# Attention of a two-layer decoder trunk: transposed weights kept and 64 value columns streamed, the division by the sums put on the results, each pair of heads turned back by transposes

## The chip, the cores and the metric

The kernel runs on one NeuronCore of one Trainium2 chip. The metric is the device time of one execution in microseconds; the time before is the median of three runs. The engines are named as in the profile: PE is TensorE (its weight loads are PEld), DVE is VectorE, ACT is ScalarE, POOL is GpSimd, SP is SyncE.

## The reference

The program is a whole two-layer trunk on 512 tokens of width 1024. The change lies in the attention of layer 0 (8 heads, scores over 64 + 32 columns, 64 value columns a head, causal, in blocks of 128 queries):

```python
def mla_attention(qn, qr, kn, kr, v):
    S = qn.shape[1]
    scale = 1.0 / math.sqrt(QK_NOPE + QK_ROPE)
    outs = []
    for i in range(S // Q_BLOCK):
        q0, k_end = i * Q_BLOCK, (i + 1) * Q_BLOCK
        s = (jnp.einsum("bqhd,bkhd->bhqk", qn[:, q0:k_end], kn[:, :k_end])
             + jnp.einsum("bqhr,bkr->bhqk", qr[:, q0:k_end], kr[:, :k_end]))
        s = s.astype(jnp.float32) * scale
        mask = (q0 + jnp.arange(Q_BLOCK))[:, None] >= jnp.arange(k_end)[None, :]
        s = jnp.where(mask, s, jnp.finfo(jnp.float32).min)
        p = jax.nn.softmax(s, axis=-1).astype(v.dtype)
        outs.append(jnp.einsum("bhqk,bkhd->bqhd", p, v[:, :k_end]))
    o = jnp.concatenate(outs, axis=1)
    return o.reshape(o.shape[0], S, MLA_HEADS * V_HEAD)
```

Beside it runs a convolution module on 512 channels (gate, causal depthwise convolution of width 31, layer norm, swish). The two results, 512 channels each, are concatenated and mapped by one output projection. Then come a gated MLP, layer 1 (a pooling mixer and a second MLP) and a last norm.

## The kernel before

Activations are kept transposed: channels on the 128 partitions, the 512 tokens along the free dimension. Products with weights are made in three parts (`mm3`, L106 to L109): every fp32 operand is split into a high and a low half (`split`, L95 to L97: ACT casts the high half, DVE subtracts it to get the low one), and high × high, high × low and low × high are summed in one PSUM bank. The attention itself (L491 to L551) works in plain fp32.

For each head, `scores` (L491) makes four products, one for each block of 128 queries, 128 to 512 keys wide (L499). DVE adds the mask and takes the row maximum (L502), ACT takes the exponential and its row sum (L513), DVE takes the reciprocal of the four sums (L518), and ACT multiplies the four blocks of weights by it (L520). `transposes` (L524) turns the ten 128x128 blocks of weights on PE (L534), and ACT copies them out of PSUM into `pt` (L536), whose part j holds the weights of the keys in block j, turned, for all queries from block j on. `values` (L540) makes four products: the loaded operand is `vals[j]`, 128 keys by the 128 value columns of the head and its neighbour in the pair; the streamed one is part j of `pt`, 512, 384, 256 and 128 columns. The result has value columns on partitions and tokens along the free dimension. Of its 128 rows the 64 that belong to the head are split (L551) into its half of the pair's tile `att[hp]`.

The loop over heads (L572) interleaves three heads: scores of head h, transposes of h − 1, queries of h + 2 and values of h − 2. In between, `pump` hands out pieces of the depthwise convolution: a tap is either a product with a diagonal matrix on PE (L380) or a multiply-add on DVE (L387). After the loop stand the values of head 6, the first part of the output projection (`half`, L588; products with `att[0]` to `att[2]`), the transposes of head 7, more of the projection, and then the layer norm of the convolution's result: four rounds of transposes on PE (L612) into two banks used in turn, statistics on DVE (L614, L615), a copy on ACT (L617). The values of head 7 (L619) and the products with `att[3]` follow in the code, then rsqrt (L624, helper at L190), normalise (L626), four rounds of transposes back (L637), swish on ACT (L639) and the split, whose results enter the rest of the output projection.

That is the order in the code. The tile framework then orders the instructions of each engine itself by dependencies and its own costs, so the order on an engine differs from the code; each engine works through its own list in that order. PSUM results of the attention take banks in turn from a pool of six (`bank`, L82). The four closing copies of the convolution (`close`, L400 to L402) stand on ACT: the last, `side_876` before and after, is what the last transposes of each round at L612 read. Weights come by DMA in one stream (L121), and each arriving piece is split into halves by ACT and DVE (`prepare`, L142).

Of the kernel before, what the change touches and what calls it, by code (L numbers as in the profile page):

```python
# [8 lines left out]
F32 = mybir.dt.float32  # L9
F32R = mybir.dt.float32r  # L10
I32 = mybir.dt.int32
AF = mybir.ActivationFunctionType
# [3 lines left out]
P = 128  # L16
# [28 lines left out]
def kernel(  # L45
# [20 lines left out]
    act, dve, pool, pe = nc.scalar, nc.vector, nc.gpsimd, nc.tensor  # L66
# [11 lines left out]
    def uid(s):  # L78
        count[0] += 1
        return f"{s}{count[0]}"  # L80

    def bank():  # L82
        return p_ps.tile([P, S], F32, tag="ps", name=uid("ps"))

    def aux(tag="aux"):
        return p_ps.tile([P, S], F32, tag=tag, bufs=1, name=uid(tag))
# [4 lines left out]
    def small(n=4, dt=F32):  # L91
        return p_s.tile([P, 8], dt, tag=f"s{dt}", name=uid("s"))[:, :n]


    def split(dst, src):  # L95
        i = act.copy(dst[0], src)  # L96
        dve.tensor_tensor(dst[1], src, dst[0].bitcast(F32), op=ALU.subtract)  # L97
        return i
# [12 lines left out]
    def pair(t, lo=0, hi=S):  # L111
        return t[:, 0, lo:hi], t[:, 1, lo:hi]
# [4 lines left out]
    def rows_of(t, a, b):  # L117
        return t[a:b, 0, :], t[a:b, 1, :]
# [35 lines left out]
    def weights(ahead=1):  # L154
        given[0] += 1
        while len(ready) < min(given[0] + ahead, len(stream)):
            prepare()
        w = ready[given[0] - 1]
        ready[given[0] - 1] = None
        return w  # L160
# [4 lines left out]
    spare = p_s.tile([P, 1], F32, tag="spare", bufs=1, name="spare")  # L165
    dve.memset(spare, 1.0)
    act.activation(spare, spare, AF.Copy)
    ps = bank()
# [11 lines left out]
    ident, ones, fold_kr = sq[:, 0, :], sq[:, 1, :], sq[:, 2, :]  # L180
# [170 lines left out]
    def project():  # L351
        w = weights()
        ps = bank()
        for k in range(KD):
            mm3(ps, part(w, k), pair(xg[k]), k == 0, k == KD - 1)
        return ps
# [52 lines left out]
    def pump(nd, np_=0):  # L409
        for _ in range(min(np_, len(pe_work))):  # L410
            pe_work.pop(0)()
        for _ in range(min(nd, len(work))):
            work.pop(0)()
# [16 lines left out]
    def s4():  # L430
        return p_m.tile([P, 2, S], F32R, tag="s4", bufs=8, name=uid("s4"))
# [16 lines left out]
    ps = project()  # L448
# [14 lines left out]
    p_a = tc.alloc_tile_pool(name="attn", bufs=1, side="right", reuse_waits="tile")  # L463
# [13 lines left out]
    qs, probs, pts, sums, att = {}, {}, {}, {}, []  # L477
# [13 lines left out]
    def scores(h):  # L491
        q, key = qs.pop(h), keys[h // 2 % 2][:, h % 2, :]
        pb = p_a.tile([P, 1280], F32, tag="prob", bufs=3, name=uid("prob"))
        mx, nb, ls = small(), small(), small()
        blocks, at = [], 0
        for i in range(4):
            w = (i + 1) * P
            ps = bank()
            pe.matmul(ps[:, :w], q[:, i * P : (i + 1) * P], key[:, :w], start=True, stop=True)  # L499
            p = pb[:, at : at + w]  # L500
            at += w
            dve.tensor_tensor_reduce(  # L502
                out=p, in0=ps[:, :w], in1=causal[:, S - w :], scale=1.0,
                scalar=-3.0e38, op0=ALU.add, op1=ALU.max, accum_out=mx[:, i : i + 1],
            )
            blocks.append(p)
            if i % 2:
                two = slice(i - 1, i + 1)
                dve.scalar_tensor_tensor(
                    nb[:, two], mx[:, two], -1.0, q_scale[:, two], op0=ALU.mult, op1=ALU.mult  # L510
                )
                for n in (i - 1, i):
                    act.activation(  # L513
                        blocks[n], blocks[n], AF.Exp, bias=nb[:, n : n + 1],
                        scale=q_scale[:, n : n + 1], accum_out=ls[:, n : n + 1],
                    )
            pump(BLK, i % 2)
        dve.reciprocal(ls, ls)  # L518
        for i in range(4):
            act.activation(blocks[i], blocks[i], AF.Copy, scale=ls[:, i : i + 1])  # L520
        probs[h] = blocks
        sums[h] = ls[:, 3:4]

    def transposes(h):  # L524
        blocks = probs.pop(h)
        pt = p_a.tile([P, 1280], F32, tag="pt", bufs=2, name=uid("pt"))
        at, views = 0, []
        for js in ((0,), (1, 3), (2,)):
            ps = bank()
            n = 0  # L530
            for j in js:
                views.append((j, pt[:, at + n : at + n + S - j * P]))
                for i in range(j, 4):
                    pe.transpose(ps[:, n : n + P], blocks[i][:, j * P : (j + 1) * P], ident)  # L534
                    n += P
            act.copy(pt[:, at : at + n], ps[:, :n])  # L536
            at += n
        pts[h] = [v for _, v in sorted(views, key=lambda v: v[0])]

    def values(h):  # L540
        hp, e = h // 2, h % 2
        if e == 0:
            att.append(s4())
        ps = bank()
        for j, pt in enumerate(pts.pop(h)):
            pe.matmul(  # L546
                ps[:, j * P :], vals[j][:, hp * P : (hp + 1) * P], pt,
                start=j == 0, stop=j == 3,
            )
        a = e * 64  # L550
        split(rows_of(att[hp], a, a + 64), ps[a : a + 64, :])  # L551

    rows_kv = rows_tile()
    queries(0)
# [1 line left out]
    ps = bank()  # L556
# [7 lines left out]
    vals = []  # L564
    for j in range(4):
        ps = bank()
# [5 lines left out]
    for h in range(HEADS):  # L572
        scores(h)
        if h % 2 == 0 and h + 2 < HEADS:
            keys_of(h // 2 + 1)
        if h >= 1:
            transposes(h - 1)
        if h + 2 < HEADS:
            queries(h + 2)
        if h >= 2:  # L580
            values(h - 2)
        pump(END)
# [14 lines left out]

    last_sum = sums[HEADS - 1]
    values(HEADS - 2)
    w0 = weights()  # L600
    half(0, att, (0, 1, 2), True, w0)
    transposes(HEADS - 1)
    act.activation(spare, last_sum, AF.Silu)
    w1 = weights()
    half(1, att, (0, 1, 2), True, w1)

# [2 lines left out]
    for i in range(4):  # L609
        ps = aux(("aux", "conv")[i % 2])  # L610
# [6 lines left out]
        act.copy(yn, ps)  # L617
        yts.append(yn)
    values(HEADS - 1)  # L619
    half(0, att, (3,), True, w0)  # L620
    half(1, att, (3,), True, w1)
# [10 lines left out]
    for m in range(4):  # L632
        if m % 2 == 0:
            half(2, att, (m, m + 1), True, w2)
        ps = aux(("aux", "conv")[m % 2])
# [188 lines left out]
    for h in range(2):  # L824
        w = weights()
        for i in range(4):
            ps = aux("conv") if (h, i) == (0, 3) else bank()
# [10 lines left out]
            if (h, i) >= (0, 2):  # L838
                while zps:
                    i, ps = zps.pop(0)  # L840
# [7 lines left out]
    for m in range(KD):  # L848
        g, h = m // 2, m // 4
        ps = bank()  # L850
        for i in (0, 2, 1, 3):
            z = pair(zs[4 * h + i], (m % 4) * P, (m % 4 + 1) * P)
            q0 = min(i * P, 256)
            o = ps[:, q0 : q0 + 256]
# [136 lines left out]
```

## Time and profile before

| | before |
|---|---|
| median of 3 runs | 1016.07 us (1015.74 to 1018.9) |
| the profiled execution | 1015.51 us, span 1013.7 us |
| PE busy | 995.8 us of the span |
| DVE busy | 591.7 us |
| ACT busy | 399.7 us |
| granted TensorE clock | 0.996 |
| values, L546, 32 products | 64 passes of 128x512 to 128x128 |
| weight transposes, L534 | 80 |

The span is the time from the first to the last instruction on the core; the profiled execution's own time is 1.8 us longer. A group row of the profile gives line, engine, operation, tiles and shapes, the count, then busy time and mean of one, then the idle time before it and what ended most of that. The chain that ended last lists, for each piece of time, the instruction that the end waited for. Records of PE overlap, since an instruction's record lasts until its results are out, so what one costs in a stream is read from start to start.

### The profile page before, as it was taken

How to read it: one execution, taken by the hardware profiler on the slowest of the kernel's cores; microseconds unless marked ns; L12 is line 12 of the kernel's file. 1: busy time of each engine (PE TensorE's matmuls, PEld its weight loads, DVE VectorE, ACT ScalarE, POOL GpSimd, SP SyncE). 2: the span in 40 equal slices, each digit the busy share in tenths (PEclk: the TensorE clock that was granted, in tenths of full speed). 3: DMA queues.
4: the chain of work that ended last, by engine and by line, in shares of the span. 5: the costliest groups of instructions: out<-in, count | busy, mean ns of one | idle time of the engine just before them, and what ended most of it. 6: DMA issues, size and time to landing. Idle time of an engine off the chain costs nothing.

```text
span 1013.7 us, 11538 instructions
## 1 busy us (share of the span) xinstructions
PE 995.8 (98%) x4476; PEld 798.7 (79%) x4476; DVE 591.7 (58%) x914; ACT 399.7 (39%) x578; POOL 71.3 (7%) x107
## 2 busy tenths in 40 slices
PE   8999999999999999999999999999999999999996
PEld 6788676677888888888888889888888888888885
DVE  6999989856765555555332338485555555522323
ACT  6534677553433333333222246253333333232321
POOL 6000100022000000000000103100000000000111
PEclk9999999999999999999999999999999999999998
DMA  6432101113232232223232241322222223223212
GB/s 215 150 99 70 39 22 63 42 43 123 82 107 89 99 97 91 90 97 100 88 102 85 103 135 43 104 96 91 89 99 97 91 90 98 98 89 102 86 42 83
DMA packets 29478, 91.99 MB, mean 91 GB/s; under 512 B 4080, under 2 KB 6384, under 8 KB 29424
## 3 DMA queue, kind: packets, MB, share of 16 engines
q1 hardware_dynamic: 28880, 90.74, 27.3%
q8 instruction: 35, 0.57, 0.2%
q10 hardware_dynamic: 544, 0.52, 0.2%
q14 instruction: 19, 0.16, 0.0%
HBM read 89.02 MB, written 2.23 MB: 90 GB/s over the span
## 4 chain that ended last, share of the span: by engine, by line
PE 93%; DVE 4%; issue 1%; DMA 1%; SPq 0%; ACT 0%; DVEq 0%
PE ps L107 28%; PE ps L109 28%; PE ps L108 28%; PE ps L499 2%; PE ps L546 2%; DVE lo L97 1%; PE aux L380 1%; PE ps L534 1%; PE aux L248 1%; PE aux L226 1%; DVE xg L102 1%; DMA x<-in_xT_dram 0%; DMA col<-in_cols_dram 0%; PE ps L860 0%; PE ps L861 0%
## 5 line engine op out<-in xcount | busy, mean ns | idle before, releaser
L96 ACT CAST hi<-raw 128x1024 fp32r<-128x1024 f32 (+2 forms) x166 | 169.6, 1024 | 400.6 <-PE ps L108 373.0
L107 PE MATMUL ps<-xg,hi 128*128 128x512 f32 x816 | 324.6, 398 | 2.2 <-ACT hi L96 2.1
L109 PE MATMUL ps<-xg,lo 128*128 128x512 f32 x816 | 323.6, 397 | 1.4 <-DVE lo L97 1.4
L108 PE MATMUL ps<-xg,hi 128*128 128x512 f32 x816 | 323.8, 397 | 0.0
L97 DVE TENSOR_TENSOR lo<-raw,hi 128x1024 fp32r<-128x1024 f32 (+2 forms) x166 | 201.7, 1217 | 165.0 <-ACT hi L96 165.0
L107 PEld LDWEIGHTS ps<-xg,hi 128*128 128x128 f32 x816 | 153.9, 189 | 40.1 <-ACT hi L96 3.4
L109 PEld LDWEIGHTS ps<-xg,lo 128*128 128x128 f32 x816 | 153.7, 189 | 39.8 <-DVE lo L97 2.9
L108 PEld LDWEIGHTS ps<-xg,hi 128*128 128x128 f32 x816 | 153.9, 189 | 36.7
L107 PE MATMUL ps<-g,hi 128*128 128x512 f32 (+1 forms) x374 | 143.3, 383 | 0.0
L108 PE MATMUL ps<-g,hi 128*128 128x512 f32 (+1 forms) x374 | 143.1, 383 | 0.0
L109 PE MATMUL ps<-g,lo 128*128 128x512 f32 (+1 forms) x374 | 143.0, 382 | 0.0
L108 PEld LDWEIGHTS ps<-g,hi 128*128 128x128 f32 x374 | 70.4, 188 | 15.0
L109 PEld LDWEIGHTS ps<-g,lo 128*128 128x128 f32 x374 | 70.4, 188 | 15.0
L107 PEld LDWEIGHTS ps<-g,hi 128*128 128x128 f32 x374 | 70.4, 188 | 15.0
L687 DVE TENSOR_TENSOR t<-ps,rows 128x512 f32<-128x512 f32 x44 | 30.4, 691 | 83.8 <-PE ps L109 83.8
L699 DVE TENSOR_TENSOR t<-ps,rows 128x512 f32<-128x512 f32 x44 | 30.4, 690 | 75.0 <-PE ps L109 75.0
L213 POOL TENSOR_TENSOR sqr<-sqr,sqr 128x512 f32<-128x512 f32 x33 | 51.0, 1545 | 321.6 <-ACT sqr L211 291.5
L387 DVE SCALAR_TENSOR_TENSOR conv<-u,col,conv 128x512 f32<-128x512 f32 x90 | 67.5, 750 | 1.6 <-ACT conv L370 0.5
L694 DVE SCALAR_TENSOR_TENSOR t<-t,col,t 128x512 f32<-128x512 f32 x88 | 65.7, 748 | 1.4
L697 ACT ACTIVATE t<-t 128x512 f32<-128x512 f32 x44 | 27.8, 631 | 74.2 <-DVE t L694 74.2
L102 DVE SCALAR_TENSOR_TENSOR xg<-x,col,xg 128x512 fp32r<-128x512 f32 x32 | 32.7, 1038 | 12.1 <-ACT xg L101 12.1
L107 PE MATMUL ps<-s,hi 128*128 128x512 f32 x96 | 39.1, 421 | 0.0
(180 smaller groups left out, 812.9 us busy)
## 6 DMA issues: line engine op xcount, KB each, us to landing
raw<-in_w_up_dram SPq DMA_DIRECT2D x88, 512.0 KB, 3.3
raw<-in_w_down_dram SPq DMA_DIRECT2D x44, 512.0 KB, 3.2
raw<-in_w_in_dram SPq DMA_DIRECT2D x10, 512.0 KB, 3.3
raw<-in_w_out_dram SPq DMA_DIRECT2D x8, 512.0 KB, 3.3
x<-in_xT_dram SPq DMA_DIRECT2D x8, 256.0 KB, 4.2
raw<-in_w_in_dram SPq DMA_DIRECT2D x8, 256.0 KB, 3.6
raw<-in_w_uq_dram SPq DMA_DIRECT2D x4, 384.0 KB, 3.0
out_dram<-g SPq DMA_DIRECT2D x6, 256.0 KB, 2.6
```

The lines of the kernel that those rows point to most:

```text
L96: i = act.copy(dst[0], src)
L97: dve.tensor_tensor(dst[1], src, dst[0].bitcast(F32), op=ALU.subtract)
L102: dve.scalar_tensor_tensor(dst[1], src, scale, dst[0].bitcast(F32), op0=ALU.mult, op1=ALU.subtract)
L107: pe.matmul(ps, a[0], b[0], start=start, stop=False)
L108: pe.matmul(ps, a[0], b[1], start=False, stop=False)
L109: pe.matmul(ps, a[1], b[0], start=False, stop=stop)
L213: self.engine.tensor_tensor(self.parts[0], self.parts[0], t, op=ALU.add)
L387: i = dve.scalar_tensor_tensor(st["acc"], u[m][:, j : j + S], c(cw + j), st["acc"], op0=ALU.mult, op1=ALU.add,)
L687: dve.tensor_tensor(ut[:, 2 : 2 + S], pu, rows, op=ALU.mult)
L694: dve.scalar_tensor_tensor(a, ut[:, j : j + S], c(fw + j * NF + f), a, op0=ALU.mult, op1=ALU.add)
L697: act.activation(a, a, AF.Silu)
L699: dve.tensor_tensor(b, pv, rows, op=ALU.mult)
```

## The change

The weights are no longer multiplied by the reciprocal sums; they are turned unscaled. In `values` the loaded operand is now the 128x128 block of turned weights, and the streamed one the head's 64 value columns: ten products a head, one for each pair of a query block i and a key block j ≤ i, the products of one i summed in 64 columns of a bank. The result has tokens on partitions, so the reciprocal sum of a row is a per-partition scale, and ACT applies it while it copies the four results into the pair's tile `o`. After the second head of a pair PE turns `o` back by four transposes into one bank, and the pair is split once, at full height.

```diff
         dve.reciprocal(ls, ls)
-        for i in range(4):
-            act.activation(blocks[i], blocks[i], AF.Copy, scale=ls[:, i : i + 1])
         probs[h] = blocks
-        sums[h] = ls[:, 3:4]
+        sums[h] = ls
...
+    outs = {}
+
     def values(h):
+
+
         hp, e = h // 2, h % 2
         if e == 0:
+            outs[hp] = p_a.tile([P, 4, P], F32, tag="o", bufs=2, name=uid("o"))
+        o, pt, ls = outs[hp], pts.pop(h), sums[h]
+        ps = bank()
+        for i in range(4):
+            for j in range(i + 1):
+                pe.matmul(
+                    ps[:, i * 64 : i * 64 + 64], pt[j][:, (i - j) * P : (i - j + 1) * P],
+                    vals[j][:, h * 64 : h * 64 + 64], start=j == 0, stop=j == i,
+                )
+        for i in range(4):
+            act.activation(
+                o[:, i, e * 64 : e * 64 + 64], ps[:, i * 64 : i * 64 + 64], AF.Copy,
+                scale=ls[:, i : i + 1],
+            )
+        if e:
+            ps = bank()
+            for i in range(4):
+                pe.transpose(ps[:, i * P : (i + 1) * P], o[:, i, :], ident)
             att.append(s4())
-        ps = bank()
-        for j, pt in enumerate(pts.pop(h)):
-            pe.matmul(
-                ps[:, j * P :], vals[j][:, hp * P : (hp + 1) * P], pt,
-                start=j == 0, stop=j == 3,
-            )
-        a = e * 64
-        split(rows_of(att[hp], a, a + 64), ps[a : a + 64, :])
+            split(pair(att[hp]), ps)
...
-    act.activation(spare, last_sum, AF.Silu)
+    act.activation(spare, last_sum[:, 0:1], AF.Silu)
```

In the changed program the values are L550, the scaling L555, the turning back L562, and later lines stand 13 further down (the transposes of the convolution's rows are L625 instead of L612); `transposes` stands two lines higher (L532 and L534 instead of L534 and L536).

Since the framework orders the instructions anew, three places are shown as they stand in the two programs. The first is PE at the values of heads 5 and 6. Before, from the end of the transposes of head 6:

```order
L534 MATMUL ps_1597<-sq,prob_1477 128x128 x2
L546 MATMUL ps_1601<-pt_1518,v_967 128x512
L546 MATMUL ps_1601<-pt_1518,v_976 128x384
L546 MATMUL ps_1601<-pt_1518,v_985 128x256
L546 MATMUL ps_1601<-pt_1518,v_994 128x128
L546 MATMUL ps_1622<-pt_1584,v_967 128x512
L546 MATMUL ps_1622<-pt_1584,v_976 128x384
```

Now, from the ninth and tenth products of head 5 (`ps_1625`) on; `ps_1640` is the bank into which pair 2 is turned back, and `ps_1662` holds the values of head 6:

```order
L550 MATMUL ps_1625<-v_985,pt_1538 128x64
L550 MATMUL ps_1625<-v_994,pt_1538 128x64
L562 MATMUL ps_1640<-sq,o_1555 128x128
L550 MATMUL ps_1662<-v_967,pt_1608 128x64
L562 MATMUL ps_1640<-sq,o_1555 128x128
L550 MATMUL ps_1662<-v_967,pt_1608 128x64
L562 MATMUL ps_1640<-sq,o_1555 128x128 x2
L550 MATMUL ps_1662<-v_976,pt_1608 128x64
```

The four transposes of the pair stand between the first products of the next head. At pairs 0 and 1 the ten products of the second head are followed by one conv tap (L380) and then by the four transposes.

The second place is PE behind the values of head 7. Before, `ps_1785` and `ps_1635` to `ps_1680` are banks of the output projection, `s_1621` is `att[3]`:

```order
L546 MATMUL ps_1740<-pt_1655,v_976 128x384
L546 MATMUL ps_1740<-pt_1655,v_985 128x256
L546 MATMUL ps_1740<-pt_1655,v_994 128x128
L107 MATMUL ps_1785<-s_1220,hi_1675 128x512
L108 MATMUL ps_1785<-s_1220,hi_1675 128x512
L109 MATMUL ps_1785<-s_1220,lo_1676 128x512
L107 MATMUL ps_1785<-s_1392,hi_1675 128x512
L107 MATMUL ps_1635<-s_1621,hi_1376 128x512
L107 MATMUL ps_1636<-s_1621,hi_1376 128x512
L107 MATMUL ps_1679<-s_1621,hi_1631 128x512
L107 MATMUL ps_1680<-s_1621,hi_1631 128x512
L612 MATMUL aux_1700<-sq,side_454 128x128
```

Now, from the turning back on, which stands directly behind the ten products of head 7 (`att[3]` is `s_1808`):

```order
L562 MATMUL ps_1803<-sq,o_1661 128x128 x4
L107 MATMUL ps_1849<-s_1312,hi_1723 128x512
L108 MATMUL ps_1849<-s_1312,hi_1723 128x512
L109 MATMUL ps_1849<-s_1312,lo_1724 128x512
L107 MATMUL ps_1849<-s_1498,hi_1723 128x512
L107 MATMUL ps_1683<-s_1808,hi_1380 128x512
L107 MATMUL ps_1684<-s_1808,hi_1380 128x512
L107 MATMUL ps_1727<-s_1808,hi_1679 128x512
L107 MATMUL ps_1728<-s_1808,hi_1679 128x512
L108 MATMUL ps_1849<-s_1498,hi_1723 128x512
L109 MATMUL ps_1849<-s_1498,lo_1724 128x512
L625 MATMUL aux_1748<-sq,side_454 128x128
```

Two more matmuls of the projection stand ahead of the transposes of the convolution's rows, beside the four transposes of the pair.

The third place is ACT at the same point, with the engines that each row waits for. Before, from the copies of the turned weights of head 7 to the closing copy of the convolution:

```order
L536 COPY pt_1655<-ps_1656 128x512 [waits PE_49]
L536 COPY pt_1655<-ps_1662 128x512 [waits PE_49]
L536 COPY pt_1655<-ps_1668 128x256 [waits PE_49]
L96 CAST s_1621<-ps_1740 64x512 [waits PE_49]
L402 ACTIVATE side_876<-aux_1011,col 128x512 [waits DVE_49]
```

Now:

```order
L534 COPY pt_1703<-ps_1704 128x512 [waits PE_49]
L534 COPY pt_1703<-ps_1710 128x512 [waits PE_49]
L534 COPY pt_1703<-ps_1716 128x256 [waits PE_49]
L555 ACTIVATE o_1661<-ps_1788,s_1574 128x64 [waits PE_49]
L555 ACTIVATE o_1661<-ps_1788,s_1574 128x64 [waits Activation_49] x3
L96 CAST s_1808<-ps_1803 128x512 [waits PE_49]
L402 ACTIVATE side_876<-aux_1011,col 128x512 [waits DVE_49]
```

The four scalings have come in ahead of the cast, and only the first of them names PE.

## The prediction

> **What bounds the kernel now.** I read the page first: the engines' totals and the summary of the chain that ended last.
>
> ```profile
> PE 995.8 (98%) x4476; PEld 798.7 (79%) x4476; DVE 591.7 (58%) x914; ACT 399.7 (39%) x578; POOL 71.3 (7%) x107
> PE 93%; DVE 4%; issue 1%; DMA 1%; SPq 0%; ACT 0%; DVEq 0%
> ```
>
> TensorE bounds the whole; 93% of the chain is PE, 4% DVE. The change lies between the first and the last weighted sum of values, so I cut the span by stages (engine busy us; the table by stretches):
>
> ```profile
> 129.50:189.20 59.70, 59.70 (x258) 41.16 (x257) 55.52 (x120) 41.40 (x96) 3.62 (x6) 1.00 0.08 27
> 189.20:204.20 15.00, 12.90 (x66) 9.31 (x66) 11.13 (x29) 8.49 (x13) 0.10 (x1) 1.00 0.26 79
> 204.20:1013.70 809.50, 799.16 (x3595) 651.18 (x3594) 413.86 (x550) 282.08 (x355) 47.29 (x73) 1.00 0.28 92
> ```
>
> In the first stretch, the attention, PE is busy all 59.70 us at clock 1.00, with DVE close behind (55.52) and ACT at 41.40. In the second, the hand-over to the output projection, PE has 2.10 us of holes. A busy PE can hide waits, because records overlap, so I looked at the pitch from start to start, which the chain in order of time gives:
>
> ```profile
> 146.23 1.09 PE ps L534 x10
> 149.41 2.16 PE ps L546 x8
> 152.23 0.86 PE aux L380 x2
> ```
>
> Ten transposes take 1.09 us (0.109 each), one head's values 2.16, one conv tap 0.86. The same three figures come back for every head, with 0.23 for each weight matmul. So PE never waits in the attention: its time there is a sum of pitches, and each pitch added is added to the run. The third view is the chain behind the last values:
>
> ```profile
> 187.02 2.16 PE ps L546 x8
> 189.18 0.23 PE ps L107
> ...
> 189.87 1.17 PE ps L107 x5
> 191.04 0.44 PE aux L612 x4
> ...
> 194.20 1.02 DVE lo L97
> ...
> 199.72 0.56 DVE t L626
> ...
> 202.06 0.79 ACT t L639
> 202.85 0.04 issue
> 202.89 0.66 PE aux L637 x4
> ```
>
> Up to the first transposes of the conv rows (L612, 191.04) it is PE's own order. From there it runs over DVE (statistics, rsqrt, normalise) and ACT back to PE, and PE's other matmuls are only filler. So what moves L612 moves the end.
>
> **What leaves ACT and DVE.** The groups of ACT by form (count, busy us, mean ns of one):
>
> ```profile
> L520 ACT ACTIVATE prob<-prob,s 128x512 f32<-128x512 f32 x8 | 5.7, 711 | 0.0
> L520 ACT ACTIVATE prob<-prob,s 128x384 f32<-128x384 f32 x8 | 4.8, 603 | 0.0
> L520 ACT ACTIVATE prob<-prob,s 128x256 f32<-128x256 f32 x8 | 4.0, 497 | 0.0
> L520 ACT ACTIVATE prob<-prob,s 128x128 f32<-128x128 f32 x8 | 3.2, 402 | 0.7 <-DVE s L518 0.6
> L536 ACT COPY pt<-ps 128x512 f32<-128x512 f32 x16 | 8.6, 580 | 2.3 <-PE ps L534 2.3
> L536 ACT COPY pt<-ps 128x256 f32<-128x256 f32 x8 | 3.0, 371 | 0.0
> L570 ACT ACTIVATE v<-ps,s 128x512 f32<-128x512 f32 x4 | 2.7, 687 | 2.9 <-PE ps L109 2.9
> L96 ACT CAST hi<-raw 128x1024 fp32r<-128x1024 f32 x6 | 6.3, 1048 | 3.3 <-PE ps L108 3.3
> ```
>
> And from the timeline, four scalings in a row and the last head's split:
>
> ```profile
> 178.65 1.93 ACT L520 ACTIVATE prob<-prob,s 128x128 f32<-128x128 f32 x4
> 189.21 0.58 ACT L96 CAST s<-ps 64x512 fp32r<-64x512 f32 x1 [5.88 <-PE ps L546]
> 189.83 0.69 DVE L97 TENSOR_TENSOR s<-ps,s 64x512 fp32r<-64x512 f32 x1 [0.93 <-ACT s L96]
> ```
>
> The scaling of the weights goes: 5.7 + 4.8 + 4.0 + 3.2 = 17.7 us of ACT. Eight half-height splits become four of full height and 512 columns like these, so 4 × 0.58 of ACT and 4 × 0.69 of DVE go too. I value all of it at zero: PE waited for none of it (its pitches are whole). The sums that are now kept whole, and the copy that reads them at L603, cost nothing more. A gain below zero is excluded in the attention for that reason; in the hand-over the chain enters DVE only behind L612.
>
> **What PE gets for its values.** Before: 8 × 2.16 = 17.3 us. After, each head has ten products of 64 columns; in fp32 a product is two passes (the chain shows eight passes for four products), each loading 128 columns of transposed weights. So 160 passes. No row of the kernel before has 64 columns. The nearest below are the sums of squares, 128 columns loaded and only 2 streamed:
>
> ```profile
> 69.35 0.95 PE L226 MATMUL aux<-sq,sqr 128*128 128x2 f32 x8
> 70.15 0.48 PE L107 MATMUL ps<-xg,hi 128*128 128x512 f32 x1
> 70.47 0.40 PE L108 MATMUL ps<-xg,hi 128*128 128x512 f32 x1
> ```
>
> From the first start (69.35) to L108 (70.47) less one L107 pitch (0.23) are 0.89 us for 8 passes, 0.111 each. A pass that streams next to nothing costs as much as one transpose with 128 columns: the load sets the pitch. The chain itself books less, as the load of the next matmul then shows in the 0.32 us from L107 to L108:
>
> ```profile
> 69.51 0.79 PE aux L226 x8
> ```
>
> That is 0.099 each, the small end of the near rows. The far end: if only streamed columns counted, 512 + 384 + 256 + 128 = 1280 columns in two passes took 2.16 us, 0.84 ns a column and pass, so 64 columns 0.054 us. I take 0.111, as both a 2-column and a 128-column neighbour show about that. One head: 20 × 0.111 = 2.22, **+0.06 a head, +0.5 us** in all. The far end would be 20 × 0.054 = 1.08 a head, −8.6 us.
>
> [...]
>
> **The turning back.** 4 pairs × 4 transposes × 0.109 = **+1.7 us** on PE, by the pitch; one record is longer, since records overlap:
>
> ```profile
> L534 PE MATMUL ps<-sq,prob 128*128 128x128 f32 x80 | 10.0, 273 | 0.0
> ```
>
> They take one more of the six result banks a pair; PE waited for no bank before, so I put that at zero, and its price if the cover is gone is in the third rival. [...]
>
> **The new wait.** The transposes need the four scaled results. On ACT the first of the four waits for PE and the others do not, so I take it that it waits for the whole bank of values, not for its own 64 columns. Its price: L570 reads PSUM with a scale, 687 ns at 512 columns; the slope of the copies is (580 − 371)/256 = 0.82 ns a column, so 64 columns cost 0.32 us (estimate). Four in a row overlap as L520's do, (2.21 − 1.93)/3 = 0.09 each: 1.0 us. ACT starts 0.28 us after PE's stream has left the values (L107 started at 188.93, the cast at 189.21):
>
> ```profile
> 188.93 0.48 PE L107 MATMUL ps<-s,hi 128*128 128x512 f32 x1
> 189.82 0.69 ACT L402 ACTIVATE side<-aux,col 128x512 f32<-128x512 f32 x1
> ```
>
> and PE follows ACT by 0.04 (202.85 above). With E the end of the values on PE, the four results are there at E + 0.65, 0.88, 1.11, 1.33. Last pair: nothing stands between, the last transpose ends at E + 1.44 and holds 0.44 of work: 1.0 us lost. Pair 2: each transpose is followed by one product of the next head (0.22), so only the first wait is lost, 0.65. Pairs 0 and 1: a tap of 0.86 stands between; 0.15 each. Sum **+1.95 us**. Behind the waiting transposes everything on PE is queued. Bounds: 0.35 if each result waited for its own columns only, and 1.05 more a pair if a weight cast (1048 ns above) stood ahead on ACT.
>
> The cast of the last pair (E + 1.5 to 2.1) and the closing copy L402 (to 2.8) come behind on ACT; L612 stands on PE at E + 1.44 + 10 × 0.23 = 3.8. Both are covered by the matmuls between; with less than 1 us of them L402 would decide.
>
> **The order.** In the hand-over ten weight matmuls now stand between the values and L612 where eight stood: **+0.47 us** before the chain goes to DVE. The fillers behind are shorter by as much, but nothing waits for them.
>
> **Sum.** 0.5 + 1.7 + 1.95 + 0.47 = 4.6 us, carried unchanged through the third stretch, where PE is busy 799 of 809 us. The profiled execution took 1015.51 us (span 1013.7 and 1.8 around it), which becomes 1020.1. It lies 0.56 under the median of the runs, 1016.07; on that the forecast is **1020.7 us**, 0.45% slower. About 0.3%, 3 us, is what a measurement of this kernel can tell from no change.
>
> **Rivals.**
> - *Streamed columns set the pass, faster.* If loads hide behind other passes, values cost 1.08 a head: −8.6 + 1.7 + 1.95 + 0.47 = −4.5, 1011.6 us. It decides once a pass costs under 0.082 us (160 × 0.029 = 4.6). For it: 512- and 384-column passes hide their loads. Against: L226 at 0.111. Chance 0.06.
> - *The small ends, no change.* A pass at the 0.099 that the chain books (−1.4), transposes 1.7, half of the waits because ACT starts each result on its own columns, 1.0, order 0.47: +1.8, 1017.9 us. For it: the waits are estimates, and ACT has 18.3 us free in the 59.7. Chance 0.18.
> - *ACT's order makes it late, slower still.* If at each pair a cast or the exponentials stand ahead of the four scalings, each wait grows by about 1.05: +8.8, 1024.9. Against: ACT loses 17.7 us there and the casts stand beside the values' 2.2 us. DVE, in order too, stops at the pair's split until the cast is there, and the next scores' reduction waits behind it; its slack is 4.2 us. Chance 0.08.
> - That the change is not made is excluded: the order shows eighty products of 64 columns.
>
> The forecast keeps 0.68, with its own range from 1019.2 (waits 1.0, a pass a little cheaper) to 1022.4 (pairs 0 to 2 each 0.6 later). The range 1017.8 to 1023.0 takes in the second rival and leaves out the first and the third. Slower by over 0.3% means over 1019.1: 0.62 of the forecast's 0.68 and all of the third, 0.70. Within 0.3%: 0.06 and 0.18, 0.24. Faster: 0.06.
>
> **What would show it.** In the profile after: values of a head as 20 passes in 2.1 to 2.3 us from start to start; 16 transposes at 0.109; PE idle or stretched before them by about 1.0 at the last pair, 0.65 at the one before; L612 4 to 5 us later than 191.04 and the stretch behind it as long as before. Wrong if the values take under 1.7 us a head, if PE waits in the attention for DVE or for a free bank, or if the distance from L612 to the first output matmul of L639's results changes.

## The result and the profile after

The changed kernel takes 1021.86 us, median of 6 runs (1021.03 to 1022.52), beside 1015.81 us (1014.54 to 1018.9) for the kernel before on the same chip: ratio 1.0059, 95% interval 1.0048 to 1.0070. It is slower, as forecast, 1.2 us above the predicted 1020.7 and inside the range. The profiled execution took 1021.94 us with a span of 1020.1 us, 6.4 us more than before. One thing of single executions is needed below: the mean granted clock was 0.990 to 0.992 in five of the six executions after and 0.994 in one, while of the 79 executions of the kernel before that stood beside the experiments 63 had 0.993 to 0.997 (median 1016.1 us) and 16 had 0.991 (median 1018.2 us).

The engines' totals and the clock in 40 slices, from the page of the kernel after:

```profile
PE 1000.7 (98%) x4588; PEld 808.2 (79%) x4588; DVE 589.0 (58%) x910; ACT 390.3 (38%) x574; POOL 71.3 (7%) x107
PEclk9999999989999999999999999999999999999998
```

PE has 4.9 us more work, ACT 9.4 us less (by rows 17.7 us of scaling and 2.3 us of half-height casts gone, 7.4 us of scaled copies come in; rows overlap, so they don't add up to the total). The ninth slice, about 204 to 230 us, has an 8 where before there was none: the first thing that the forecast hadn't. The table by stretches, cut as before (attention, hand-over, rest):

```profile
129.30:192.50 63.20, 62.39 (x370) 49.54 (x368) 52.91 (x116) 36.35 (x101) 3.62 (x6) 1.00 0.08 26
192.50:208.60 16.10, 13.64 (x67) 10.21 (x67) 11.35 (x29) 8.65 (x14) 0.10 (x1) 0.91 0.26 78
208.60:1020.10 811.50, 801.12 (x3596) 651.96 (x3595) 413.60 (x550) 281.84 (x355) 47.36 (x73) 0.99 0.27 91
```

PE, full in the attention before, now has 0.81 us without work there, and the hand-over runs at a mean clock of 0.91. The chain in order of time shows the pieces:

```profile
129.43 2.18 PE ps L550 x20
...
141.82 0.44 PE ps L562 x4
...
174.00 2.19 PE ps L550 x20
176.22 0.32 ACT o L555
...
176.59 0.33 PE ps L562
...
189.19 2.19 PE ps L550 x20
191.41 0.32 ACT o L555
...
191.78 0.94 PE ps L562 x4
...
195.06 0.44 PE aux L625 x4
...
206.21 0.79 ACT t L652
...
207.04 1.12 PE aux L650 x4
```

Twenty passes of 64 columns take 2.18 us, where eight of up to 512 columns took 2.16. ACT's scaling is now in the chain at the last two pairs and not at the first two (141.82: four transposes in 0.44, no wait). The last line has four transposes in 1.12 us; before, the same four took 0.66.

To see where the time came in, I read four starts on PE in each trace: the first product of the values; the first transpose of the conv rows into the bank `aux` (L612 before, L625 after); the first transpose back (L637, L650); and the next sum of squares (L226), at about 256 us.

| distance, us | before | after | difference |
|---|---|---|---|
| first values to conv rows | 61.46 | 65.62 | +4.16 |
| conv rows to transposes back | 9.53 | 9.54 | +0.01 |
| transposes back to sum of squares | 55.37 | 57.71 | +2.34 |
| from there to the end | 757.9 | 757.9 | 0 |

So 4.16 us came in the attention and at its end, the chain over DVE is as long as it was, and 2.34 us came behind it, where the change has moved nothing. There the clock is seen in a table by stretches of the kernel after:

```profile
194.90:202.50 7.60, 7.60 (x40) 5.95 (x38) 6.21 (x16) 4.08 (x7) 0.00 (x0) 1.00 0.24 74
202.50:205.90 3.40, 1.59 (x8) 0.80 (x8) 3.16 (x12) 1.01 (x1) 0.00 (x0) 0.98 0.44 142
205.90:212.40 6.50, 5.84 (x19) 4.68 (x19) 3.48 (x5) 4.84 (x8) 0.10 (x1) 0.50 0.25 83
212.40:222.00 9.60, 9.60 (x43) 7.71 (x42) 0.00 (x0) 0.00 (x0) 0.00 (x0) 0.99 0.00 0
```

For 3.40 us PE has run out of projection matmuls and does a few transposes, busy 1.59 us; then TensorE is granted half its clock for 6.5 us. The nearest stretch of the profiled execution before is not answered so:

```profile
199.10:204.10 5.00, 2.90 (x18) 1.68 (x17) 3.59 (x9) 2.91 (x5) 0.10 (x1) 1.00 0.31 104
204.10:212.00 7.90, 7.90 (x36) 6.41 (x35) 2.54 (x4) 2.81 (x5) 0.00 (x0) 1.00 0.15 56
```

In this trace the granted clock is 1.00 or 0.50 and nothing else, and PE was not idle ahead of the lower one, busy 1.59 of 3.40 us. Whether the same hole could lose the clock in one execution and keep it in another is taken up behind the last experiments.

### The profile page after: what moved, and what is told of

Read it like the earlier page. It is cut to its first block, busy times and chain, and to the rows that moved or that the text cites. A ratio compares the mean times of both kernels' runs of the same rounds, so it can differ in the third digit from the quotient of the medians.

```text
span 1020.1 us, 11755 instructions
## 1 busy us (share of the span) xinstructions
PE 1000.7 (98%) x4588; PEld 808.2 (79%) x4588; DVE 589.0 (58%) x910; ACT 390.3 (38%) x574; POOL 71.3 (7%) x107
## 4 chain that ended last, share of the span: by engine, by line
PE 93%; DVE 4%; issue 1%; DMA 1%; SPq 0%; ACT 0%; DVEq 0%
PE ps L107 28%; PE ps L109 28%; PE ps L108 28%; PE ps L499 2%; PE ps L550 2%; DVE lo L97 1%; PE aux L380 1%; PE ps L532 1%; PE aux L248 1%; PE aux L226 1%; DVE xg L102 1%; DMA x<-in_xT_dram 0%; DMA col<-in_cols_dram 0%; PE ps L874 0%; PE ps L873 0%
## 5 line engine op out<-in xcount | busy, mean ns | idle before, releaser
L97 DVE TENSOR_TENSOR lo<-raw,hi 128x1024 fp32r<-128x1024 f32 (+2 forms) x166 | 201.7, 1216 | 165.0 <-ACT hi L96 165.0
```

## The experiments

My theory after the result: the load of the weights sets a pass with 64 columns streamed (0.109 us), as with 2 (0.111) and 128 (0.109) in the kernel before (values +0.6), 16 transposes cost 1.75, the last two pairs wait for ACT, two more matmuls stand ahead of the conv rows; and the rest is the clock, which falls because PE's hole in the hand-over got emptier. Rivals: the ACT relief or the width decides; the extra 2.3 us are not the clock but the new traffic of `o`; the hand-over's order, which the framework chose, is worth more than all the arithmetic of the change. Distances as in the table above, in us; each ratio is to runs of the kernel before on the same chip, whose median was 1015.81 to 1016.60 us, so ratios and distances compare across the table better than the medians do:

| kernel | median us (runs) | ratio to before, 95% | values to rows | rows to back | back to squares |
|---|---|---|---|---|---|
| e_noscale | 1015.89 (11) | 0.9998 (0.9989–1.0008) | 61.46 | 9.53 | 55.38 |
| e_nowait | 1022.62 (4) | 1.0059 (1.0044–1.0075) | 66.10 | 9.84 | 56.93 |
| e_late | 1019.94 (5) | 1.0036 (1.0023–1.0049) | 63.45 | 11.52 | 56.14 |
| e_fill | 1020.26 (5) | 1.0037 (1.0024–1.0049) | 65.64 | 9.45 | 55.46 |
| e_hole | 1017.35 (11) | 1.0010 (1.0001–1.0019) | 61.47 | 11.24 | 56.50 |
| e_wide | 1016.69 (10) | 1.0001 (0.9992–1.0010) | 59.68 | 11.37 | 56.12 |
| e_order | 1018.80 (10) | 1.0023 (1.0009–1.0038) | 61.38 | 11.46 | 56.13 |
| a_lo | 1018.69 (11) | 1.0022 (1.0013–1.0031) | 65.62 | 8.41 | 55.61 |
| a_both | 1018.09 (10) | 1.0019 (1.0005–1.0034) | 61.37 | 11.48 | 56.13 |
| b_lo | 1014.72 (11) | 0.9981 (0.9972–0.9990) | 61.46 | 8.41 | 55.61 |
| b_order | 1016.10 (10) | 0.9996 (0.9984–1.0008) | 60.25 | 11.34 | 56.13 |
| b_both | 1015.94 (10) | 0.9996 (0.9985–1.0007) | 60.25 | 10.32 | 56.12 |

**e_noscale: ACT's relief alone.** The kernel before without the scaling:

```diff
-        for i in range(4):
-            act.activation(blocks[i], blocks[i], AF.Copy, scale=ls[:, i : i + 1])
```

> The kernel before without the 32 scalings of the weights by the reciprocal sums on ACT (17.7 us of ACT); it leaves out the division. Theory: PE waited for none of them, so the time is that before within 0.3 us. Rival (the relief of ACT is worth something that the change then gives back): 1 us or more faster.

Every distance is that of before to 0.01 us, and the ratio 0.9998. Taking the 17.7 us of scalings off ACT (its total falls from 399.7 to 385.4 us) is worth nothing, as valued.

**e_nowait: the transposes without their wait.** In the kernel after, the turning transposes read a tile that has long been there:

```diff
-                pe.transpose(ps[:, i * P : (i + 1) * P], o[:, i, :], ident)
+                pe.transpose(ps[:, i * P : (i + 1) * P], vals[i][:, :P], ident)
```

> The changed kernel whose 16 turning transposes read the value tiles, long ready, in place of the scaled results; it leaves out the use of the attention's result behind the scaling. The framework puts 15 projection matmuls, not 10, ahead of the conv rows in the hand-over, so the stretches are to be read apart. Theory: from the first product of values to the last transpose of pair 3 the trace loses the 1.2 us of waits and keeps the 1.75 us of transposes at 0.109 each. Rival (the transposes themselves are dear, 0.2 us or more each, and nothing waits): that stretch stays as long as in the changed kernel.

The ratio is that of after, 1.0059, and the clock falls in the hand-over here too (0.50 in 206 to 212 us, 0.95 in the 6 us ahead). The expected loss is there, from the first values to the end of the last transpose 61.93 us instead of 63.45, but it doesn't reach the end. PE at the last pair, from the timeline of this kernel:

```profile
189.04 2.34 PE L550 MATMUL ps<-v,pt 128*128 128x64 f32 x20
191.22 0.61 PE L562 MATMUL ps<-sq,v 128*128 128x128 f32 x4
192.40 0.50 PE L107 MATMUL ps<-s,hi 128*128 128x512 f32 x1 [0.57 <-ACT o L555]
```

and in the kernel after:

```profile
189.03 2.34 PE L550 MATMUL ps<-v,pt 128*128 128x64 f32 x20
191.78 0.94 PE L562 MATMUL ps<-sq,o 128*128 128x128 f32 x4 [0.41 <-ACT o L555]
192.47 0.48 PE L107 MATMUL ps<-s,hi 128*128 128x512 f32 x1
```

The transposes follow the values at once, but the next matmul of the projection then stands behind ACT for almost as long: 192.40 instead of 192.47. At pair 2 the wait does go: from the first product of head 5 to the projection are 4.78 us (174.36 to 179.14) instead of 5.30 (173.84 to 179.14), that is 0.52 less. The order on PE changed with it, too: fifteen matmuls stand ahead of the conv rows instead of ten, 1.17 us, which eats the gain. So the wait at the last pair is not the transposes' alone; ACT's four copies cost it in either form, though which bank or tile the projection's matmul waits for was not followed.

**e_late: the transposes away from their wait.** The turning of pairs 0 and 1 comes after the next head's scores, that of pair 2 after the values of head 6, that of pair 3 behind the conv rows, and with it the products with `att[3]`:

```diff
+        if h >= 4 and h % 2 == 0:
+            turn(h // 2 - 2)
...
+    turn(2)
...
-    half(0, att, (3,), True, w0)
-    half(1, att, (3,), True, w1)
...
+    with tc.issue_after(behind_conv.ins):
+        turn(3)
+    half(0, att, (3,), True, w0)
+    half(1, att, (3,), True, w1)
```

> The changed kernel with each pair turned back later: pairs 0 and 1 after the next head's scores, pair 2 behind the values of head 6, pair 3 behind the last transposes of the conv rows, with the products that need it behind that. The framework then puts the transposes of the conv rows directly behind the values of head 7. Theory: the waits of the turning back (1.2 us), its last four transposes (0.44) and the ten projection matmuls ahead of the conv rows (2.3 us) leave the path, and the chain to the end starts some 3 to 4 us earlier; with a shorter hole no drop of the clock: 1016 to 1018 us. Rival: the matmuls that were fillers are now late and bound PE behind the chain, or the closing copy of the last conv row is not ready (DVE's taps): 1019 to 1021.

The conv rows come 2.17 us sooner (63.45 for 65.62) and the chain behind them is 1.98 longer. PE now waits for the closing copy of the convolution, which ACT makes behind the four scalings:

```profile
193.64 1.07 PE L629 MATMUL aux<-sq,side 128*128 128x128 f32 x4 [1.59 <-ACT side L402]
```

This is the cover that the prediction named ("with less than 1 us of them L402 would decide"), now gone: the 1016 to 1018 us that I expected were missed, and the rival of the closing copy came true. The clock falls right behind it, from the table by stretches:

```profile
193.90:200.70 6.80, 5.61 (x22) 4.81 (x21) 4.50 (x14) 2.83 (x5) 0.00 (x0) 0.51 0.00 0
```

**e_fill: work in the hole.** The kernel after, with thirty small bf16 matmuls on a tile of zeros issued ahead of the first transposes back:

```diff
+        if m == 0:
+            for _ in range(30):
+                pe.matmul(ps[:, :P], idle, idle, start=True, stop=True)
```

> The changed kernel with 30 small bf16 products of zeros put among PE's fillers of the hand-over (their result is overwritten by the transposes of the normalised rows), about 1.7 us of PE work that nothing waits for. Theory: 2.3 of the 6 us that the change costs are the TensorE clock, which the trace after grants at 0.50 from 205.9 to 212.4 us behind a longer hole of PE; with the hole filled the clock stays at 1.00 there, the mean clock goes back to 0.996, and the time falls by 1.8 to 2.3 us, to about 1019.7. Rival: the stretch is long because the four transposes and the first products wait for ACT and DVE; then the filler changes nothing (1021.9) or adds up to 1.7 us.

The framework put them ahead of the last projection matmuls, which so came later and filled the hole. The table by stretches of this kernel, over the same times:

```profile
202.00:205.90 3.90, 3.49 (x31) 2.74 (x28) 3.45 (x17) 0.00 (x0) 0.00 (x0) 1.00 0.79 251
205.90:212.40 6.50, 5.71 (x31) 4.17 (x30) 4.24 (x8) 5.88 (x9) 0.10 (x1) 1.00 0.26 83
```

Clock 1.00, and the distance behind the chain is 55.46, 2.25 less than after; its mean granted clock is 0.994 to 0.996 in all five runs. The median fell by 1.6 us, and the ratio from 1.0059 to 1.0037, which is 2.2 us. In its profiled execution the clock was low near the start, in 10 to 30 us (0.91), which the profiled execution after hadn't. So the 2.34 us are the clock to within 0.1 us, and the traffic of `o` is not needed to explain them.

**e_hole: the hole made in the kernel before.** One more DVE operation in the chain:

```diff
+    dve.tensor_scalar(yts[0], yts[0], 1.0, None, op0=ALU.mult)
```

> The kernel before with one more pass of DVE over the first of the four normalised rows (times 1.0), about 0.5 us in the chain from the statistics to the transposes, so that PE's hole there is as long as in the changed kernel. Theory of the clock: the hole, not the new way of making the values, drops the clock; the granted clock falls to 0.50 for some us behind it and the time grows by 0.5 + 2.3, to about 1018.6, mean clock about 0.992. Rival (the drop belongs to the new values and transposes): +0.5 us, 1016.3, and a mean clock of 0.996.

The operation's record is 0.42 us, yet the chain got 1.71 longer. In DVE's order it stands behind all four normalise steps (201.88, the first of them at 200.05), and the first transpose back, which could follow the first step before, now waits for it. So PE's hole is 3.01 us, longer than the 1.77 in the kernel after. The clock fell in the profiled execution, and for as long:

```profile
202.00:208.40 6.40, 5.93 (x22) 4.95 (x23) 3.02 (x5) 4.75 (x8) 0.10 (x1) 0.50 0.27 84
```

The median, 1017.35, is only 0.1% above before and 1.3 below the expected 1018.6, and only two of the eleven executions have the expected mean clock of 0.992. The trace shows the drop without the change, but before has such executions too, so how often the hole calls it up is not shown, and with the chain made longer at once the test doesn't price it.

**a_lo and b_lo: a shorter chain, in both.** In the chain between conv rows and transposes back, DVE also made the low halves of weights for the projection (the line `DVE lo L97` of the chain before). They now come behind the last normalise:

```diff
-        copied = split((hi, lo), raws[i])
+        copied = act.copy(hi, raws[i])
+        with ExitStack() as late:
+            if lo_after:
+                late.enter_context(tc.issue_after(lo_after[0]))
+            dve.tensor_tensor(lo, raws[i], hi.bitcast(F32), op=ALU.subtract)
```

> The kernel before with the low halves of the three weight tiles that are prepared in the hand-over taken by DVE behind the normalising instead of among the statistics; PE's order stays. Theory: the chain from the transposes of the conv rows (L612) to those back is bound by DVE's order, of which two splits of 1.2 us are part; without them it is up to 2.2 us shorter, then bound by PE's own fillers, so about 1.4 us go, the hole of PE closes and the clock cannot drop: about 1015, and no execution with the mean clock of 0.991. Rival (the splits are needed as soon for the products behind, or statistics wait for PE): no change.

> The same in the changed kernel. Theory: the chain is up to 2.2 us shorter and the hole closes, so that the clock stays at 1.00 behind it: 1.4 to 2.2 plus 2.3 us less than the changed kernel, 1017.5 to 1018.2. Rival (the drop of the clock does not hang on the hole): the gain stays under 2.2 us, 1019.7 or more.

The chain got 1.12 us shorter in both, 8.41 us, and behind it the clock is 1.00 in both traces; none of b_lo's eleven executions has a mean clock under 0.994. b_lo takes 1014.72 us, less than both kernels of this case and near the expected 1015. a_lo takes 1018.69, 0.5 above the expected range and 3.2 less than after; by the distances 1.13 are the chain and 2.10 the clock (55.61 for 57.71). With the clock thus alike, the change costs 1018.69 − 1014.72 = 3.97 us, and by the distances 4.16, all of it ahead of the conv rows: this is what the prediction's 4.6 us stood for.

**e_wide: 128 columns streamed.** The kernel after with the neighbour's columns streamed too and thrown away:

```diff
-                    ps[:, i * 64 : i * 64 + 64], pt[j][:, (i - j) * P : (i - j + 1) * P],
-                    vals[j][:, h * 64 : h * 64 + 64], start=j == 0, stop=j == i,
+                    ps[:, i * P : (i + 1) * P], pt[j][:, (i - j) * P : (i - j + 1) * P],
+                    vals[j][:, hp * P : (hp + 1) * P], start=j == 0, stop=j == i,
```

> The changed kernel with the 128 value columns of the pair streamed in each product in place of the head's 64, of which ACT still takes 64; the results are the same. Theory: the load of 128 columns sets a pass, so a head's 20 passes stay at 2.2 us from start to start. Rival (streamed columns set the pass, with some fixed cost): 64 more columns at 0.84 ns a column and pass, 1.1 us more a head, 8.6 us in all.

On the width the chain of this kernel is plain:

```profile
175.01 2.25 PE ps L550 x20
...
190.03 0.44 PE aux L625 x4
...
190.57 1.34 PE ps L550 x12
...
194.95 0.73 PE ps L562 x3
```

Twice the columns take 2.25 us instead of 2.18, where 1.1 us more were due if streamed columns set the pass: the load, 128 columns in both, sets it (0.112 and 0.109 us a pass). But the run as a whole is 5.2 us faster than after, level with before. The lines show what else is new: the conv rows (L625) now stand ahead of the values of head 7, and the projection's matmuls, which in the kernel after stood ahead, fill the chain behind them. The framework had chosen another order for the hand-over. That called for the next four.

**e_order, b_order, a_both, b_both: that order given to the others.** In the kernel after, before, a_lo and b_lo the values of head 7 are held behind the first round of conv rows:

```diff
+        if i == 0:
+            conv_row = behind_conv
...
-    values(HEADS - 1)
+    with tc.issue_after(conv_row.ins):
+        values(HEADS - 1)
```

> The kernel after (64 value columns) with its last head's values held behind the conv rows, which is the order on TensorE that the kernel with 128 columns had got; nothing else is changed. Theory, order: the 5.2 us between the kernel after and the one with 128 columns are the hand-over (the projection matmuls stand behind the last values and cover the chain of conv rows, no hole, clock at 1.00), so this kernel comes out where that one did: about 1016.7 us (1016.0 to 1017.5), 127.0 us from the first values product to the next sum of squares. Rival, width: half the columns make the values dearer, or the order costs nothing; then it stays at 1020 to 1022 us, with 131 to 133 us in that stretch.

> The kernel before with its last head's values held behind the conv rows in the same way; nothing else is changed. Theory, order: its TensorE is idle for 2.1 us in 186 to 206 us, and the same order fills most of that: 1.3 to 2 us less than before, about 1014.3 us, ratio 0.998 to 0.9985. Rival: the stretch is set by the chain of conv rows on VectorE and ScalarE, which gets longer as the values' split comes into it: ratio 0.9995 to 1.001.

> The kernel before with that order and with the three low halves of the weights moved behind the last normalise. If the order leaves TensorE no idle time, the shorter chain gives nothing more: 1014 to 1014.5 us, as each of the two alone. If the chain still ends last, the two gains add up: 1013 us, ratio 0.9965.

> The kernel after with both edits. By the theory of the order no hole is left, so it equals the kernel with the order alone, about 1016.5 us, and stays some 2 to 2.5 us above the kernel before with the same two edits (transposes 1.75, waits that the last pairs keep, passes 0.6). By the rival that the change is free once the hand-over is mended, both come out within 0.5 us of each other.

e_order came out between the two theories: 1018.80. The three distances together are 132.87 us after, 128.97 in e_order and 127.17 in e_wide, so the order gave 3.9 of 5.7 us (3.1 of 5.2 by the medians), among them the clock that after loses, and 1.8 stay between e_order and e_wide, with the same order on PE from the first conv rows in `aux` on. The place is the conv rows, in the timeline of e_order:

```profile
181.42 9.45 DVE L387 SCALAR_TENSOR_TENSOR aux<-u,col,aux 128x512 f32<-128x512 f32 x12
190.91 0.69 ACT L402 ACTIVATE side<-aux,col 128x512 f32<-128x512 f32 x1 [4.56 <-DVE aux L387]
191.65 0.33 PE L625 MATMUL aux<-sq,side 128*128 128x128 f32 x1 [1.46 <-ACT side L402]
```

and in that of e_wide:

```profile
180.83 5.50 DVE L387 SCALAR_TENSOR_TENSOR aux<-u,col,aux 128x512 f32<-128x512 f32 x7
186.43 0.71 ACT L402 ACTIVATE side<-aux,col 128x512 f32<-128x512 f32 x1
189.86 0.60 PE L625 MATMUL aux<-sq,side 128*128 128x128 f32 x4
```

At the end of the attention twelve conv taps in a row are left for DVE in e_order, seven in e_wide, where the framework had put more of them earlier in DVE's list. The rows need the last tap (190.87 against 186.33), so in e_order PE waits 1.46 us for them, and the distance from the values to the rows is 1.70 longer. That the taps' place is most of the remaining 1.8 us is read from the traces; no kernel moved the taps alone.

b_order gains nothing for the same reason, more strongly. In its timeline PE stands still for 2.66 us:

```profile
189.29 0.98 PE L612 MATMUL aux<-sq,side 128*128 128x128 f32 x4 [2.66 <-ACT side L402]
```

The 2.1 us of holes that I meant to fill are paid there instead, so my expectation for it fell. b_both, 1015.94, is not better than b_lo either, where 1013 to 1014.5 was expected; the gains don't add up. These two have the same hole on PE, and answer it differently. The table by stretches of b_order:

```profile
186.00:189.40 3.40, 0.74 (x6) 0.41 (x5) 2.41 (x4) 0.69 (x1) 0.00 (x0) 1.00 0.00 0
189.40:192.80 3.40, 3.40 (x11) 2.21 (x12) 1.51 (x4) 1.17 (x2) 0.00 (x0) 0.51 0.00 0
```

and of b_both:

```profile
186.00:189.40 3.40, 0.85 (x6) 0.47 (x4) 2.63 (x4) 0.63 (x1) 0.00 (x0) 1.00 0.00 0
189.40:192.80 3.40, 2.85 (x16) 1.85 (x17) 2.04 (x5) 1.23 (x3) 0.00 (x0) 1.00 0.00 0
```

PE is busy for 0.74 and 0.85 of 3.40 us; behind it one has the clock at 0.51 for 3.4 us and the other at 1.00, and b_order's chain is 1.02 us longer (11.34 for 10.32). Of that, 0.87 lie between the first conv row and the first projection matmul behind the values (5.24 for 4.37, the same matmuls), where the clock is low; the late low halves, the other difference, gave nothing between e_order and a_both (11.46 and 11.48). So a nearly empty hole cost the clock in one of the two and not in the other.

A lead is in the traces too, which hold the times at which the granted clock changed. In that of after it changed at 205.76, 212.59 and 1011.31 us, which lie 6.83 and 798.72 us apart, 2 and 234 times 3.413; the record of the clock begins at 4.38, 59 times 3.413 ahead of the first change. In that of before the record begins at 5.62 and the only change, at 1005.73, comes 293 times 3.413 later. So I cut the traces into windows of 3.413 us that end on such changes. b_order's hole fills one window (186.06 to 189.47, PE busy 0.75 us). In b_both it lies across two:

```profile
184.45:187.86 3.41, 2.40 (x12) 1.71 (x11) 3.27 (x5) 0.00 (x0) 0.00 (x0) 1.00 0.00 0
187.86:191.28 3.42, 1.63 (x7) 0.80 (x7) 1.91 (x4) 1.03 (x2) 0.00 (x0) 1.00 0.00 0
```

From 1.00 the clock fell behind the windows with PE busy 0.75 us (b_order), 0.93 (before, 1002.31 to 1005.73), 1.60 (after, 202.35 to 205.76), 1.70 (after, 1007.90 to 1011.31) and 1.81 (e_late, 190.50 to 193.91, a cut that runs 0.2 us into the fall). It stayed behind 1.63 (b_both), 1.67 and 1.80 (before, 32.93 to 36.35 and 12.45 to 15.86) and 1.97 (after, 14.62 to 18.03), and behind every fuller window of before and after. Between 1.63 and 1.81 us, then, either was seen. In after it stayed at 0.50 behind a first low window with PE busy 2.77 us (205.76 to 209.18) and came back behind a second that was full (3.41); in b_order the first was full already, and the drop lasted 3.4 us there and 6.8 in after.

Between a_both and b_both, with the same two edits, are 2.15 us: the price of the change where the order is kept alike and hides part of the waits.

## Why the prediction was right, and where its sum was off

The sign was right, and so was the size up to the conv rows, by the steps that were named; one term was missing and one too large:

| term, us | predicted | in the profile after |
|---|---|---|
| values, eight heads | +0.5 | +0.6: 2.18 for 2.16 in the chain, and 0.05 more behind each head |
| turning back, 16 × 0.109 | +1.7 | +1.75 (0.44 for four, at 141.82) |
| wait, pairs 0 and 1 | +0.30 | 0 |
| wait, pair 2 | +0.65 | +0.50 |
| wait, pair 3 | +1.0 | +0.82 |
| ten matmuls for eight | +0.47 | +0.47 |
| chain from conv rows to transposes back | 0 | +0.01 |
| third stretch | 0 | +2.34 |

The wait at pair 3 is the distance from the first values to the next projection matmul, 189.03 to 192.47, 3.44, less 2.18 and 0.44; at pair 2, 5.30 less twice 2.18 and 0.44. The rows down to the order add up to 4.14, and the distance grew by 4.16.

- *What bounds it* held: each pitch added on PE in the attention was added to the run, and ACT's relief was worth nothing (e_noscale). DVE's was not tried alone.
- *What PE gets for its values* held: the rival by which streamed columns set the pass falls with 2.18 us for twenty passes, and e_wide shows 2.25 with twice the columns.
- *The new wait* was of the right kind and too large, 1.32 for 1.95. The four scalings took 0.93 us for the estimated 1.0, ACT began 0.20 us behind PE's stream (191.41 against 189.03 + 2.18) and not 0.28, and at pairs 0 and 1 the tap hid it all, where 0.15 each was set. That ACT waits for the whole bank was right: its first scaling starts at 191.41, and the record of the last pass ends at 191.37 (189.03 + 2.34). The third rival, ACT late at each pair, falls with the pairs 0 and 1.
- *The step that failed* is "carried unchanged through the third stretch": the sum was carried, and 2.34 us came on top, because the clock halved for two windows, 6.8 us, after the hole (0.50 from 205.76 to 212.59). One of the prediction's own signs of being wrong told of it: the distance from L612 to the first output matmul behind the transposes back went from 13.2 to 13.8 us. The prediction saw holes of 2.10 us in the hand-over and wrote of the shorter fillers that "nothing waits for them". For the chain that was right, it is 0.01 longer; what it missed is that the clock fell where fewer fillers stood, and stayed at 1.00 where e_fill put thirty more. Two fewer of them stood behind the rows, and the window over the hole had PE busy 1.60 us (202.35 to 205.76); before, the hole lay across two windows with 2.35 and 2.37. e_fill and a_lo each take it away in a different manner, and the third stretch is then 55.46 and 55.61, as before.

The forecast missed by less than this term, 1.8 us on the profiled executions (1021.94 against 1020.1), because the waits had been set 0.6 too high; that the two errors partly cancel is luck, and the upper part of the range had been set for later waits, not for the clock. What stays open is the edge: between 1.63 and 1.81 us of busy records windows went either way, and no run here varies only how full it is. That every execution after loses the clock in the hand-over is not shown either: only one was profiled, and a mean clock can't tell it, since the traces of e_late and e_order both have 0.994, the one with the drop there and the other without.

## What to carry to other kernels

Price a narrow fp32 product by the weights it loads, not by the columns it streams: here twenty passes took 2.18 us with 64 columns and 2.25 with 128, so nothing was left to gain, and turning the result back is all loss. Where a framework orders the instructions, an edit upstream can reorder a hand-over, and that can outweigh the edit (5.2 us here, the clock included, for an edit that adds streamed columns), so compare two versions with the order held alike before crediting the edit. Before moving fillers, look at what PE does in the hole they leave: thirty matmuls that nothing waited for went with a clock of 1.00 in e_fill, where after had 0.50, and with 2.25 us less.

## What the runs showed of the hardware that I had not expected

- In the traces of before and after the granted clock changed only at whole multiples of 3.413 us from where its record begins (293; 59, 61 and 295). It fell to 0.50 behind windows of that length with PE busy 0.75 us (b_order) and 1.60 (after), and in e_late behind one with 1.81. In the hand-over it was at 0.50 for 6.8 us in after, e_hole and e_late, for at least 6 us in e_nowait and for 3.4 us in b_order. In the kernel after this cost 2.1 to 2.3 us. A run's mean clock hardly tells it, 0.992 in after and 0.996 before: five other traces (a_both, e_fill, e_hole, e_noscale, e_order) have a drop between 10 and 30 us (mean clock 0.91 there), and before and after end with 8.0 and 8.8 us at 0.50.
- A pass loading 128 fp32 columns took, from start to start, 0.111 us with 2 columns streamed (L226, before), 0.109 with 64 (L550, after) and 0.109 to 0.112 with 128 (transposes, before; L550, e_wide). The thirty bf16 matmuls of e_fill, also 128 by 128, took half of that:

```profile
201.17 1.85 PE L651 MATMUL aux<-idle 128*128 128x128 bf16 x30
202.82 0.48 PE L108 MATMUL ps<-s,hi 128*128 128x512 f32 x1
```

From 201.17 to 202.82 are 1.65 us, 0.055 each. Between 202 and 203 us the trace has 18 weight loads (PEld), busy all of the 1.00 us, so the loads ran at that pitch too. All thirty name the same tile for both operands; whether the type or the repeated tile makes the difference wasn't tried.
